# The combined projection without its normalised input, and the lower bound's factor moved to the queries

## The chip, the cores and the metric

The kernel runs on one core of a Trainium2 chip. The metric is device time in microseconds (us), the median of several runs; lower is better. Where a profile is read, it is that of a single execution. PE is the matrix engine, PEld its weight loads, DVE the vector engine, ACT the scalar engine, POOL the general engine (GpSimd), SP the engine that here only issues transfers. A letter q behind a name is that engine's queue.

## The reference

One layer of a bidirectional hybrid encoder on x (1, 512, 1024) with memory tokens (1, 256, 1024), all float32. The part that matters here is the first sub-layer:

```
h = rmsnorm(x, pre_mix_g)
aq, ak, av, hq, hf_fwd, hf_bwd, hi, hg = split_columns(h @ w_in, IN_SPLITS)
aq, ak = rmsnorm per head of 64 with q_norm_g, k_norm_g, then 2-D rotary
att = axial_gqa_attention(aq, ak, av)
# HGRN2 group, 4 heads of 128:
q = silu(hq)
f_dir = lb_dir + (1 - lb_dir) * sigmoid(zf_dir)      # forward and backward
k_dir = 1 - f_dir                                    # = (1 - lb_dir) * sigmoid(-zf_dir)
o = bidirectional_gated_scan(q, log f_fwd, log f_bwd, hi)
rec = rmsnorm(o, out_g) * silu(hg)
x = x + rmsnorm(concat(att, rec) @ w_out, post_mix_g)
```

A root-mean-square norm multiplies each row (token) of x by one number r and each column by a gain. The gain can go into the input of the projection, and r can be applied to the projection's output. Then follow a cross-attention into the memory, whose rows are normalised with mem_norm_g, and a gated MLP.

## The kernel before

Every matrix product is made of three matmuls, because both operands are held as a rounded part (hi, in code wh or hi) and a rest (lo, wl): hi by hi, hi by lo, lo by hi (`mm3`, L143 to L146). 132 units of weights of 128 x 1024 come in a fixed order, each through one raw buffer (2 of them) into wh and wl (4 buffers each). `issue` (L115) makes a unit: the plain way is a cast on ACT and a subtraction on DVE (`split`, L102); units in NEG_SCALAR (4 to 27) get a cast on ACT (L121), a negation on ACT (L123), and a second transfer of the same weights on POOL's queue that adds them to the negation (L126); units in NEG_POOL (28 to 41) are negated on POOL. `unit` (L137) hands out the next unit and issues up to AHEAD = 3 units beyond those taken; `hold` (L131) is an upper limit for that.

The instructions of each engine run in the order that a planner gave them when the kernel was built; it follows the order of the text, but an instruction that the plan sees ready earlier can be put ahead. `tc.issue_after(i)` puts instructions behind i on i's engine. `weave` (L57) mixes several streams of text by their progress.

The start, in order:

- L338 to L376: x arrives transposed in eight chunks of 128 columns, is multiplied by the gain of its columns and split into `raw_act` (the input without r), while units 0 to 3 are split; the projection of the values v (column group hi) runs on PE (L375) from `raw_act`.
- L386 to L397: ACT squares and sums the rows of x (L388), POOL makes r (`rstd_of`, L160) and multiplies the identity by it into `diag_r` (L392), PE spreads r over all partitions by multiplying with ones (L395), ACT copies that into `r_bc` (L397).
- L400: `normalize` makes the normalised input: gain and r on DVE (L402), then a split (ACT L103, DVE L104) into `hT`. It is called for chunks 0 to 7 between the matmuls of head 0 (L671 to L673).
- L439: `put_v` multiplies v's rows by r on ACT as they leave the accumulators, ahead of head 0's projections.
- `hgrn_in(h)` (L459): three projections of a head, one unit each: q (silu: L465, L466), then the gates f and the keys k of both directions (`put_f`, L468 to L476). Head 0 reads `raw_act`, and its results are multiplied by r_bc on DVE (`scaled`, L442 to L446). Heads 1 to 3 read `hT`.
- `mix_projections` (L654): `mem_norm` (L639), which loads the memory's gain and rows on POOL's queue (L157, L644), squares the rows on ACT (L197) and scales them on DVE (L179); then the projection of the output gate (`put_sg`, L449: sigmoid on ACT, the gain out_g on POOL, product on DVE), heads 1 and 2, `mem_turn`, keys and values (`put_kv`), queries (`put_qn`), head 3. With it are woven the cores 0 to 2.
- `hgrn_core(h)` (L486): the scan of a head. It begins with ksum = k_fwd + k_bwd (DVE L496) and its product with q (PE L499), and goes on in seven doubling steps, each with a copy on ACT (L506), matmuls (L509), products on DVE (L535) and a masked copy (L541), then further steps; at the end the head's output is normalised, multiplied by the gate (L559), turned and split into `mix`.

Accumulator banks go by tags of two buffers each: b (head projections), c (cores), s and o (gate, keys, queries). Sixteen large buffers of 8 KB a partition (`big`, tag big) hold activations.

Of the kernel before, what the change touches and what calls it, by code (L numbers as in the profile page):

```python
# [18 lines left out]
P = 128  # L19
# [54 lines left out]
def layer(tc, io, out):  # L74
# [30 lines left out]

    pending, last_pow = deque(), [None]
    issued, taken, last_load = [0], [0], [None]
# [35 lines left out]
    def mm3(o, a, b, start, stop):  # L143
        nc.tensor.matmul(o, a[0], b[0], start=start, stop=False)  # L144
        nc.tensor.matmul(o, a[0], b[1], start=False, stop=False)  # L145
        nc.tensor.matmul(o, a[1], b[0], start=False, stop=stop)  # L146

# [11 lines left out]

    def rstd_of(ss, n, width):  # L160
        r = small()
        nc.gpsimd.tensor_scalar(r[:, :n], ss, 1.0 / width, EPS, op0=ALU.mult, op1=ALU.add)
        last_pow[0] = nc.gpsimd.tensor_tensor(out=r[:, :n], in0=r[:, :n], in1=nhalf[:, :n], op=ALU.pow).ins
        return r
# [172 lines left out]

    raw_act = new_act()  # L338

    after = []  # L340

    def split_x(kc):
        src = xt[kc // 4][:, kc % 4, :]
        hi, lo = raw_act.get(kc, slice(0, T))
# [18 lines left out]
    for j in range(4):  # L363
        if j >= 2:
            w_raw.append(load_w())
        wh = wp.tile([P, 1024], F32R, name="wh", tag="wh")
        wl = wp.tile([P, 1024], F32R, name="wl", tag="wl")
        for k in range(2):
            in_turn(split_x, 2 * j + k)
            in_turn(split_w, wh[:, half(k)], wl[:, half(k)], w_raw[j][:, half(k)])  # L370
        for k in range(2):
            kc = 2 * j + k
            for a, w in ((0, wh), (0, wl), (1, wh)):
                for b in range(NB):
                    nc.tensor.matmul(v_ps[b], raw_act.get(kc, blk(b))[a], w[:, half(k)],  # L375
                                     start=kc == 0 and a == 0 and w is wh, stop=kc == 7 and a == 1)  # L376
# [5 lines left out]
    taken[0] = 4  # L382
    for _ in range(2):
        issue()

    rx = const.tile([P, 2 * NB], F32, name="rx")  # L386
    for b in range(NB):
        nc.scalar.activation(tmp4([P, D]), xr[b], ACT.Square, accum_out=rx[:, b:b + 1])  # L388
    r = rstd_of(rx[:, :NB], NB, D)
    diag_r = tmp2((P, NB, P), tag="th")  # L390
    for b in range(NB):
        nc.gpsimd.tensor_scalar(diag_r[:, b, :], ident, r[:, b:b + 1], None, op0=ALU.mult)  # L392
    r_ps = bank("c")
    for b in range(NB):
        nc.tensor.matmul(r_ps[:, blk(b)], ones, diag_r[:, b, :], start=True, stop=True)  # L395
    r_bc = big([P, T])
    nc.scalar.copy(r_bc, r_ps)  # L397
    hT = new_act()

    def normalize(kc):  # L400
        t = tmp2()
        nc.vector.scalar_tensor_tensor(out=t, in0=xt[kc // 4][:, kc % 4, :], scalar=gcol[:, kc:kc + 1], in1=r_bc,  # L402
                                       op0=ALU.mult, op1=ALU.mult)
# [5 lines left out]
    og = const.tile([P, P], F32, name="og")  # L409
    cw = const.tile([P, 2 * NF, 4], F32, name="cw")  # L410
    qkg = const.tile([P, 2, 64], F32, name="qkg")
    with tc.issue_after(last_load[0]):
        nc.sync.dma_start(lbt, io["hg_lb"])
        nc.sync.dma_start(og, rows_bc(io["hg_out_norm_g"], P))
# [44 lines left out]
    def hgrn_in(h, between=(), raw=False):  # L459
        qk = big([P, 2, 2, T])  # L460
# [7 lines left out]
        def put_f(d):  # L468
            def put(z):
# [3 lines left out]
                nc.scalar.activation(k, z, ACT.Sigmoid, scale=-1.0)  # L473
                nc.vector.tensor_scalar(f, f, oml[:, d, h:h + 1], lb[:, d, h:h + 1], op0=ALU.mult, op1=ALU.add)
                nc.vector.tensor_scalar(k, k, oml[:, d, h:h + 1], None, op0=ALU.mult)
# [106 lines left out]
    def norm_rope(z, nh, which, b):  # L582
        n = nh * 64
        rope = qkv["rope"]
        u = tmp2()
        nc.scalar.activation(u[:, :n], z, ACT.Square)
        ss = small()
        nc.vector.tensor_reduce(ss[:, :nh], u[:, :n].rearrange("p (h d) -> p h d", h=nh), axis=AX.X, op=ALU.add)
        r = rstd_of(ss[:, :nh], nh, 64)
        xn = tmp2()  # L590
# [7 lines left out]
        nc.vector.tensor_add(xn[:, :n], xn[:, :n], u[:, :n])  # L598
        nc.vector.tensor_tensor(out=x3, in0=x3, in1=r[:, :nh, None].to_broadcast([P, nh, 64]), op=ALU.mult)
        return x3  # L600

    def put_kv(b, z):
# [5 lines left out]
        vv = qkv["vv"]  # L608
        split(vv[:, b, :, 0, :], vv[:, b, :, 1, :], z[:, 128:256].rearrange("p (h d) -> p h d", h=2))
        kr = norm_rope(z[:, 0:128], 2, 1, b)  # L610
# [42 lines left out]

    def mix_projections():  # L654
        mem_norm()
        yield from proj_tm(hT, tm_tags, put_sg)
        yield from hgrn_in(1)
# [359 lines left out]
```

## Time and profile before

| | |
|---|---|
| median of 3 runs | 849.56 us (848.68 to 850.97) |
| the profiled execution, its own time | 848.33 us |
| its span, first to last instruction | 846.5 us |
| granted clock of PE, mean | 0.994 |
| read from memory over the span | 100.63 MB |

A row of the timeline reads: start, duration, engine, line, operation, output<-input, shapes, and in brackets the idle time before it and what ended it. A row of the groups reads: line, engine, operation, names, shapes, count, then busy time and mean nanoseconds of one, then the idle time of the engine just before and what ended most of it. A row of the waits reads: engine, tile and line that waited, what it waited for, us in total, how often, the longest. x24 is a count.

### The profile page before, as it was taken

What the parts mean: (1) busy time and instruction counts of PE and PEld (TensorE: products, weight loads), DVE (VectorE), ACT (ScalarE), POOL (GpSimd) and SP (SyncE); (2) the same over time, 40 slices, a digit from 0 to 9 for tenths busy, and PEclk for the clock granted to TensorE, in tenths of its full rate; (3) what the DMA queues carried; (4) which work ended last, traced back from release to release, by engine and by line L of the source; (5) the groups of instructions that cost most, each with busy time, mean ns of one, the idle gap of its engine ahead of it and who ended that gap; (6) DMA issues with size and microseconds to landing.
All of it is one profiled execution on the core that took longest, in us unless ns stands there. A gap on an engine that the chain in (4) does not pass through costs nothing.

```text
span 846.5 us, 11102 instructions
## 1 busy us (share of the span) xinstructions
PE 828.5 (98%) x4304; PEld 703.5 (83%) x4304; DVE 493.2 (58%) x775; ACT 424.3 (50%) x735; POOL 107.7 (13%) x166
## 2 busy tenths in 40 slices
PE   9789999999999999999999999999999999999996
PEld 7668888988999888888888998888888888888885
DVE  5277276928987675854544865555555557722224
ACT  6764555555988774645443553333333335511121
POOL 0321411225332301300001300000000000000001
PEclk9999999999999999999999999999999999999999
DMA  8985664558677633242302242222233222222212
GB/s 320 249 220 119 143 152 94 121 129 171 152 180 167 150 103 147 85 164 75 123 27 75 93 131 100 93 90 92 100 100 99 100 101 88 99 90 96 100 50 100
DMA packets 30228, 103.45 MB, mean 122 GB/s; under 512 B 3872, under 2 KB 4512, under 8 KB 30176
## 3 DMA queue, kind: packets, MB, share of 16 engines
q1 hardware_dynamic: 22752, 77.44, 27.0%
q0 software_dynamic: 6704, 24.38, 15.4%
q10 hardware_dynamic: 720, 0.92, 0.3%
q8 instruction: 34, 0.56, 0.3%
q14 instruction: 18, 0.15, 0.1%
HBM read 100.63 MB, written 2.10 MB: 121 GB/s over the span
## 4 chain that ended last, share of the span: by engine, by line
PE 91%; DMA 4%; DVE 2%; ACT 2%; POOL 1%; issue 1%; SPq 0%; POOLq 0%; DVEq 0%; ACTq 0%
PE ps_b L146 10%; PE ps_b L144 10%; PE ps_b L145 10%; PE ps_s L146 6%; PE ps_s L145 6%; PE ps_s L144 6%; PE ps_o L144 6%; PE ps_o L145 6%; PE ps_o L146 6%; PE ps_c L144 4%; PE ps_c L145 4%; PE ps_c L146 4%; PE ps_c L509 3%; PE ps_o L727 2%; PE ps_o L715 2%; PE ps_s L705 2%
## 5 line engine op out<-in xcount | busy, mean ns | idle before, releaser
L104 DVE TENSOR_TENSOR wl<-raw,wh 128x1024 fp32r<-128x1024 f32 x90 | 110.2, 1224 | 199.5 <-ACT wh L103 199.3
L103 ACT CAST wh<-raw 128x1024 fp32r<-128x1024 f32 x90 | 94.8, 1053 | 203.7 <-PE ps_o L146 71.4
L146 PE MATMUL ps_b<-big,wl 128*128 128x512 f32 (+1 forms) x320 | 117.5, 367 | 5.1 <-DMA wl<-in_w_dram 5.1
L144 PE MATMUL ps_b<-big,wh 128*128 128x512 f32 (+1 forms) x320 | 118.6, 371 | 0.0
L145 PE MATMUL ps_b<-big,wh 128*128 128x512 f32 (+1 forms) x320 | 117.1, 366 | 0.0
L146 PEld LDWEIGHTS ps_b<-big,wl 128*128 128x128 f32 x320 | 60.7, 190 | 14.8 <-DMA wl<-in_w_dram 5.5
L172 POOL TENSOR_SCALAR small<-small 128x1 f32<-128x1 f32 x40 | 14.3, 356 | 440.4 <-ACT tmp L203 421.5
L144 PEld LDWEIGHTS ps_b<-big,wh 128*128 128x128 f32 x320 | 60.8, 190 | 9.0
L145 PEld LDWEIGHTS ps_b<-big,wh 128*128 128x128 f32 x320 | 60.7, 190 | 9.1
L121 ACT CAST wh<-raw 128x1024 fp32r<-128x1024 f32 x38 | 39.9, 1051 | 32.3 <-PE ps_b L145 14.7
L144 PE MATMUL ps_s<-wh,big 128*128 128x512 f32 (+1 forms) x140 | 54.0, 386 | 0.0
L535 DVE TENSOR_TENSOR big<-big 128x512 f32<-128x512 f32 x64 | 47.0, 741 | 10.5 <-ACT tmp L506 3.7
L146 PE MATMUL ps_s<-wh,big 128*128 128x512 f32 (+1 forms) x140 | 53.1, 379 | 0.0
L145 PE MATMUL ps_s<-wl,big 128*128 128x512 f32 (+1 forms) x140 | 53.0, 379 | 0.0
L144 PE MATMUL ps_o<-wh,big 128*128 128x512 f32 (+1 forms) x124 | 48.1, 388 | 0.0
L126 POOL DMA_DIRECT2D wl<-in_w_dram x38 | 34.2, 901 | 109.0 <-ACT wl L123 99.0
L146 PE MATMUL ps_o<-wh,big 128*128 128x512 f32 (+1 forms) x124 | 47.5, 383 | 0.0
L145 PE MATMUL ps_o<-wl,big 128*128 128x512 f32 (+1 forms) x124 | 47.3, 381 | 0.0
L104 DVE TENSOR_TENSOR big<-ps_o,big 128x512 fp32r<-128x512 f32 x52 | 35.8, 689 | 15.4 <-ACT big L103 15.1
L103 ACT CAST big<-ps_o 128x512 fp32r<-128x512 f32 x52 | 30.4, 585 | 21.3 <-PE ps_o L715 7.9
L509 PE MATMUL ps_c<-big,tmp 128*128 128x128 f32 x224 | 32.8, 289 | 4.4 <-ACT tmp L506 4.0
L144 PE MATMUL ps_b<-wh,big 128*128 128x512 f32 x92 | 36.6, 398 | 0.0
(250 smaller groups left out, 1964.2 us busy)
## 6 DMA issues: line engine op xcount, KB each, us to landing
raw<-in_w_dram SPq DMA_DIRECT2D x131, 512.0 KB, 3.3
wl<-in_w_dram POOLq DMA_DIRECT2D x38, 512.0 KB, 5.5
big<-in_x_dram SPq DMA_DIRECT2D x8, 512.0 KB, 8.0
big<-in_xt_dram SPq DMA_DIRECT2D x3, 512.0 KB, 7.6
big<-in_mem_dram POOLq DMA_DIRECT2D x2, 512.0 KB, 10.9
out_dram<-big SPq DMA_DIRECT2D x4, 256.0 KB, 2.1
out_dram<-big ACTq DMA_DIRECT2D x3, 256.0 KB, 2.1
big<-in_xt_dram SPq DMA_DIRECT2D x2, 256.0 KB, 4.0
```

Of the source, the lines that this page charges most:

```text
L103: nc.scalar.copy(hi, src)
L104: (eng or nc.vector).tensor_sub(lo, src, hi.bitcast(F32))
L121: nc.scalar.copy(wh, raw)
L126: nc.gpsimd.dma_start(wl, io["w"][i], accum_op=ALU.add)
L144: nc.tensor.matmul(o, a[0], b[0], start=start, stop=False)
L145: nc.tensor.matmul(o, a[0], b[1], start=False, stop=False)
L146: nc.tensor.matmul(o, a[1], b[0], start=False, stop=stop)
L509: nc.tensor.matmul(o[:, b, :], kc[:, blk(b)], pat(qk, b * P, [[2 * m, P // (2 * m)], [T + m, 2], [1, m]]), start=True, stop=True)
L535: nc.vector.tensor_tensor(out=c, in0=c, in1=pat(tt, toff + off, [[2, npair], [gap, 2], [0, m]]), op=ALU.mult)
L705: nc.tensor.matmul(s, qT[h // 4][:, h % 4, blk(qb)], kT[:, 2 * (h // 4) + c, :], start=c == 0, stop=c == 1)
L715: nc.tensor.transpose(o[:, c, :], e[:, 0, blk(c)], ident)
L727: nc.tensor.matmul(o, vv[:, c, h // 4].rearrange("p a d -> p (a d)"), pt[:, j, c, :], start=c + j == 0, stop=c == 3 and j == 1)
```

## The change

- `raw_act` is now called `hT` and is the only input of the combined projection; `normalize` and the second, normalised activation are gone. Everything that reads the projection applies r itself: v, the gate (scale of the sigmoid, and a factor of the product), values (`split_scaled`), the rotary norm (r goes into the square's scale and into the norm's factor, one more POOL operation), and all four heads through `scaled`, not head 0 alone.
- diag_r is multiplied on DVE, not on POOL. The spreading of r is put behind the 18th matmul of head 0's first projection (SPREAD_STEP = 2). `put_v` comes after it.
- Units 4, 5 and 6 are split by ACT and DVE; NEG_SCALAR begins at 7. Units 6 and 7 are issued behind the copy of r_bc.
- The keys k keep no factor 1 - lb. That factor (`oml`) goes to q times f, and into ksum. The gate f = lb + oml * sigmoid is formed on ACT. Half of ksum is a multiplication on ACT.
- The gain out_g leaves the gate; it is applied per partition when the head's output is split into `mix`.
- `mem_norm` comes after the gate's projection.

```diff
-NEG_SCALAR = frozenset(range(4, 28))
+NEG_SCALAR = frozenset(range(7, 28))
...
-WARM = 4
+WARM, SPREAD_STEP = 4, 2
...
+    def split_scaled(hi, lo, src, factor):
+        nc.scalar.mul(hi, src, factor)
+        nc.vector.scalar_tensor_tensor(out=lo, in0=src, scalar=factor, in1=hi.bitcast(F32), op0=ALU.mult,
+                                       op1=ALU.subtract)
...
-    raw_act = new_act()
+    hT = new_act()
...
     taken[0] = 4
-    for _ in range(2):
-        issue()
+    hold[0] = 6
+    issue_ahead()
...
-    r = rstd_of(rx[:, :NB], NB, D)
+    r = rstd_of(rx[:, :NB], NB, D, rx[:, NB:])
     diag_r = tmp2((P, NB, P), tag="th")
     for b in range(NB):
-        nc.gpsimd.tensor_scalar(diag_r[:, b, :], ident, r[:, b:b + 1], None, op0=ALU.mult)
-    r_ps = bank("c")
-    for b in range(NB):
-        nc.tensor.matmul(r_ps[:, blk(b)], ones, diag_r[:, b, :], start=True, stop=True)
+        nc.vector.tensor_scalar(diag_r[:, b, :], ident, r[:, b:b + 1], None, op0=ALU.mult)
     r_bc = big([P, T])
-    nc.scalar.copy(r_bc, r_ps)
-    hT = new_act()
-
-    def normalize(kc):
-        t = tmp2()
-        nc.vector.scalar_tensor_tensor(out=t, in0=xt[kc // 4][:, kc % 4, :], scalar=gcol[:, kc:kc + 1], in1=r_bc,
-                                       op0=ALU.mult, op1=ALU.mult)
-        split(*hT.get(kc, slice(0, T)), t)
+
+    def spread_r():
+        r_ps = bank("c")
+        with tc.issue_after(last_mm[0]):
+            for b in range(NB):
+                nc.tensor.matmul(r_ps[:, blk(b)], ones, diag_r[:, b, :], start=True, stop=True)
+        copied = nc.scalar.copy(r_bc, r_ps).ins
+        hold[0] = N_UNITS
+        with tc.issue_after(copied):
+            issue_ahead()
+        for b in range(NB):
+            put_v(b, v_ps[b])
...
-        nc.scalar.activation(s, o, ACT.Sigmoid)
-        s4 = s.rearrange("p (h n) -> p h n", h=4)
-        nc.gpsimd.tensor_tensor(out=s4, in0=s4, in1=og[:, None, :].to_broadcast([P, 4, P]), op=ALU.mult)
-        nc.vector.tensor_mul(sg_box[0][:, b, :], o, s)
+        nc.scalar.activation(s, o, ACT.Sigmoid, scale=r[:, b:b + 1])
+        nc.vector.scalar_tensor_tensor(out=sg_box[0][:, b, :], in0=o, scalar=r[:, b:b + 1], in1=s,
+                                       op0=ALU.mult, op1=ALU.mult)
...
-                nc.vector.tensor_scalar(f, f, oml[:, d, h:h + 1], lb[:, d, h:h + 1], op0=ALU.mult, op1=ALU.add)
-                nc.vector.tensor_scalar(k, k, oml[:, d, h:h + 1], None, op0=ALU.mult)
-                nc.vector.tensor_mul(qk[:, 0, 1 - d, :], q, f)
+                nc.scalar.activation(f, f, ACT.Identity, scale=oml[:, d, h:h + 1], bias=lb[:, d, h:h + 1])
+                nc.vector.scalar_tensor_tensor(out=qk[:, 0, 1 - d, :], in0=f, scalar=oml[:, d, h:h + 1], in1=q,
+                                               op0=ALU.mult, op1=ALU.mult)
...
-            yield from proj_fm(raw_act if raw else hT, T, "b", scaled(put) if raw else put)
+            yield from proj_fm(hT, T, "b", scaled(put))
...
-        nc.vector.tensor_add(ksum, qk[:, 1, 0, :], qk[:, 1, 1, :])
+        nc.scalar.mul(ksum, qk[:, 1, 0, :], oml[:, 0, h:h + 1])
+        nc.vector.scalar_tensor_tensor(out=ksum, in0=qk[:, 1, 1, :], scalar=oml[:, 1, h:h + 1], in1=ksum,
+                                       op0=ALU.mult, op1=ALU.add)
...
-        split(*mix.get(4 + h, slice(0, T)), o.rearrange("p b n -> p (b n)"))
+        split_scaled(*mix.get(4 + h, slice(0, T)), o.rearrange("p b n -> p (b n)"), og[:, 0:1])
...
-        nc.scalar.activation(u[:, :n], z, ACT.Square)
+        nc.scalar.activation(u[:, :n], z, ACT.Square, scale=r[:, b:b + 1])
...
-        r = rstd_of(ss[:, :nh], nh, 64)
+        rz = rstd_of(ss[:, :nh], nh, 64)
+        nc.gpsimd.tensor_scalar(rz[:, :nh], rz[:, :nh], r[:, b:b + 1], 0.0, op0=ALU.mult, op1=ALU.add)
...
     def mix_projections():
-        mem_norm()
         yield from proj_tm(hT, tm_tags, put_sg)
+        mem_norm()
         yield from hgrn_in(1)
...
-    for b in range(NB):
-        put_v(b, v_ps[b])
-    for i, _ in enumerate(hgrn_in(0, raw=True)):
-        if i < KC:
-            normalize(i)
+    for i, _ in enumerate(hgrn_in(0)):
+        if i == SPREAD_STEP:
+            spread_r()
```

More of the change, by code (lines that the diff above doesn't have):

```diff
@@ L104, in split @@
         (eng or nc.vector).tensor_sub(lo, src, hi.bitcast(F32))
-    pending, last_pow = deque(), [None]
+    def split_scaled(hi, lo, src, factor):
+        nc.scalar.mul(hi, src, factor)
+        nc.vector.scalar_tensor_tensor(out=lo, in0=src, scalar=factor, in1=hi.bitcast(F32), op0=ALU.mult,
+                                       op1=ALU.subtract)
+    pending, last_pow, last_mm = deque(), [None], [None]
     issued, taken, last_load = [0], [0], [None]
@@ L145, in mm3 @@
         nc.tensor.matmul(o, a[0], b[1], start=False, stop=False)
-        nc.tensor.matmul(o, a[1], b[0], start=False, stop=stop)
+        last_mm[0] = nc.tensor.matmul(o, a[1], b[0], start=False, stop=stop).ins
     def blk(b):
@@ L158, in gains, with rstd_of @@
         return [g[:, i, :] for i in range(len(names))]
-    def rstd_of(ss, n, width):
-        r = small()
+    def rstd_of(ss, n, width, r=None):
+        r = small() if r is None else r
         nc.gpsimd.tensor_scalar(r[:, :n], ss, 1.0 / width, EPS, op0=ALU.mult, op1=ALU.add)
@@ L343, in split_x @@
         src = xt[kc // 4][:, kc % 4, :]
-        hi, lo = raw_act.get(kc, slice(0, T))
+        hi, lo = hT.get(kc, slice(0, T))
         cast = nc.scalar.mul(hi, src, gcol[:, kc:kc + 1]).ins
@@ L374, in layer @@
                 for b in range(NB):
-                    nc.tensor.matmul(v_ps[b], raw_act.get(kc, blk(b))[a], w[:, half(k)],
+                    nc.tensor.matmul(v_ps[b], hT.get(kc, blk(b))[a], w[:, half(k)],
                                      start=kc == 0 and a == 0 and w is wh, stop=kc == 7 and a == 1)
@@ L408, in layer @@
     lbt = const.tile([P, 2, 2, 4], F32, name="lbt")
-    og = const.tile([P, P], F32, name="og")
+    og = const.tile([P, 1], F32, name="og")
     cw = const.tile([P, 2 * NF, 4], F32, name="cw")
@@ L413, in layer @@
         nc.sync.dma_start(lbt, io["hg_lb"])
-        nc.sync.dma_start(og, rows_bc(io["hg_out_norm_g"], P))
+        nc.sync.dma_start(og, io["hg_out_norm_g"][:, None])
         nc.sync.dma_start(masks_f, io["masks"])
@@ L452, in put_sg, with hgrn_in @@
         s = tmp2()
-        nc.scalar.activation(s, o, ACT.Sigmoid)
-        s4 = s.rearrange("p (h n) -> p h n", h=4)
-        nc.gpsimd.tensor_tensor(out=s4, in0=s4, in1=og[:, None, :].to_broadcast([P, 4, P]), op=ALU.mult)
-        nc.vector.tensor_mul(sg_box[0][:, b, :], o, s)
+        nc.scalar.activation(s, o, ACT.Sigmoid, scale=r[:, b:b + 1])
+        nc.vector.scalar_tensor_tensor(out=sg_box[0][:, b, :], in0=o, scalar=r[:, b:b + 1], in1=s,
+                                       op0=ALU.mult, op1=ALU.mult)
         sg_box.append(b)
-    def hgrn_in(h, between=(), raw=False):
+    def hgrn_in(h, between=()):
         qk = big([P, 2, 2, T])
@@ L598, in norm_rope @@
         nc.vector.tensor_add(xn[:, :n], xn[:, :n], u[:, :n])
-        nc.vector.tensor_tensor(out=x3, in0=x3, in1=r[:, :nh, None].to_broadcast([P, nh, 64]), op=ALU.mult)
+        nc.vector.tensor_tensor(out=x3, in0=x3, in1=rz[:, :nh, None].to_broadcast([P, nh, 64]), op=ALU.mult)
         return x3
@@ L608, in put_kv @@
         vv = qkv["vv"]
-        split(vv[:, b, :, 0, :], vv[:, b, :, 1, :], z[:, 128:256].rearrange("p (h d) -> p h d", h=2))
+        split_scaled(vv[:, b, :, 0, :], vv[:, b, :, 1, :], z[:, 128:256].rearrange("p (h d) -> p h d", h=2), r[:, b:b + 1])
         kr = norm_rope(z[:, 0:128], 2, 1, b)
@@ L654, in mix_projections @@
     def mix_projections():
+        yield from proj_tm(hT, tm_tags, put_sg)
         mem_norm()
-        yield from proj_tm(hT, tm_tags, put_sg)
         yield from hgrn_in(1)
```

## The prediction

> **What bounds the kernel now.** I read the page's first part, then PE's waits, then busy time by stage (in that view each row has the stretch and its length, then the busy time of PE, PE's weight loads, DVE, ACT and POOL, the granted clock, the share of the transfer engines and GB/s).
>
> ```profile
> span 846.5 us, 11102 instructions
> PE 828.5 (98%) x4304; PEld 703.5 (83%) x4304; DVE 493.2 (58%) x775; ACT 424.3 (50%) x735; POOL 107.7 (13%) x166
> ...
> PE ps_b L146 <- DMA wl<-in_w_dram: 5.1, 1, 5.1
> PE ps_c L509 <- ACT tmp L506: 4.0, 2, 3.6
> ```
> ```profile
> 0.00:20.00 20.00, 18.52 (x70) 14.70 (x70) 10.27 (x17) 12.33 (x21) 0.44 (x6) 1.00 0.88 320
> ...
> 20.00:300.00 280.00, 270.18 (x1651) 236.47 (x1650) 191.90 (x383) 188.64 (x345) 79.22 (x95) 0.99 0.67 156
> 300.00:800.00 500.00, 500.00 (x2414) 419.90 (x2413) 274.84 (x356) 213.62 (x351) 24.06 (x53) 1.00 0.29 100
> 800.00:846.00 46.00, 39.80 (x175) 32.38 (x173) 16.22 (x21) 9.73 (x20) 4.01 (x12) 0.97 0.22 78
> ```
> PE is busy 98% of the span, and from 300 to 800 us without a gap at full clock. The change leaves the number and the size of the matmuls as they are, so time can be won only where PE stands still or runs at a low clock. The stage from 20 to 300 us has 9.8 us of idle PE (280.00 - 270.18), and two waits make nearly all of it: 5.1 us for a transferred wl, and 3.6 us for a copy on ACT. The 6.2 us after 800 us are the output, which the change does not touch. So less work on DVE, ACT or POOL is worth nothing by itself: the question is what becomes of the two waits. PE's timeline around them:
>
> ```profile
> 27.93 1.05 PE L395 MATMUL ps_c<-tmp,ones 128*128 128x128 f32 x8
> 28.74 0.48 PE L144 MATMUL ps_b<-big,wh 128*128 128x512 f32 x1
> ...
> 34.51 0.80 PE L146 MATMUL ps_b<-big,wl 128*128 128x512 f32 x1 [5.06 <-DMA wl<-in_w_dram]
> ...
> 37.67 0.39 PE L144 MATMUL ps_b<-big,wh 128*128 128x512 f32 x1
> ...
> 51.76 0.39 PE L146 MATMUL ps_b<-big,wl 128*128 128x512 f32 x1
> 51.99 0.39 PE L144 MATMUL ps_s<-wh,big 128*128 128x512 f32 x1
> ...
> 55.85 1.16 PE L499 MATMUL ps_c<-tmp,tmp 128*128 128x128 f32 x8
> 60.61 1.73 PE L509 MATMUL ps_c<-big,tmp 128*128 128x128 f32 x8 [3.60 <-ACT tmp L506]
> 62.00 0.77 PE L146 MATMUL ps_o<-wh,big 128*128 128x512 f32 x1
> ...
> 65.06 0.40 PE L144 MATMUL ps_s<-wh,big 128*128 128x512 f32 x1
> ...
> 69.58 1.13 PE L509 MATMUL ps_c<-big,tmp 128*128 128x128 f32 x8 [0.41 <-ACT tmp L506]
> ```
> At full clock a 512-column matmul starts 0.227 us after the one before it (51.76 to 51.99, and so for dozens of rows). **Wait 1.** Head 0's three projections have 3 x 24 = 72 matmuls, 16.3 us at that pace; they take 51.99 - 28.74 = 23.25 us. So wait 1 costs 6.9 us: 5.06 us of standing, about 1.6 us for seven matmuls at a slow clock (34.51 to 37.67 is 3.16 us, where 7 x 0.227 = 1.59), and a remainder. **Wait 2.** It costs 3.60 us, plus 0.6 us (1.73 against the 1.13 us that the same eight passes take at 69.58), plus 62.00 to 65.06 for seven matmuls, 3.06 - 1.59 = 1.47: 5.7 us. Together 12.6 us. The short wait at 69.58 (0.41 us) is followed by the normal pace: only the long ones cost the clock too.
>
> Now what makes them, on ACT and POOL:
>
> ```profile
> 23.34 0.20 POOL L162 TENSOR_SCALAR small<-rx 128x4 f32<-128x4 f32 x1 [22.37 <-ACT tmp L388]
> 23.63 1.03 POOL L163 TENSOR_TENSOR small<-small,nhalf 128x4 f32<-128x4 f32 x1
> ...
> 27.08 1.03 POOL L126 DMA_DIRECT2D wl<-in_w_dram  x1
> ...
> 47.25 0.85 POOL L126 DMA_DIRECT2D wl<-in_w_dram  x1 [8.50 <-ACT wl L123]
> ...
> 48.36 0.85 POOL L644 DMA_DIRECT2D big<-in_mem_dram x1
> ```
> ```profile
> 23.51 1.05 ACT L121 CAST wh<-raw 128x1024 fp32r<-128x1024 f32 x1 [0.26 <-DMA raw<-in_w_dram]
> 24.59 1.06 ACT L123 ACTIVATE wl<-wh 128x1024 fp32r<-128x1024 f32 x1
> 26.30 1.05 ACT L121 CAST wh<-raw 128x1024 fp32r<-128x1024 f32 x1 [0.66 <-DMA raw<-in_w_dram]
> ...
> 58.68 1.06 ACT L197 ACTIVATE tmp<-big 128x1024 f32<-128x1024 f32 x1 [3.66 <-DMA big<-in_mem_dram]
> 59.64 0.19 ACT L197 ACTIVATION_READ_ACCUMULATOR tmp<-big 128x1 f32 x1
> 59.74 0.82 ACT L506 COPY tmp<-big 128x512 f32<-128x512 f32 x1
> ```
> Wait 1: unit 4 makes its wl by a negation on ACT (L123) and a second, adding transfer on POOL's queue (L126); that starts at 27.08, after the POOL multiplications of diag_r, and lands at 34.5. Wait 2: ACT works in order; the square of the memory rows (L197) stands ahead of core 0's first copy (L506) and waits for rows that were asked for at 48.36.
>
> **The change, part by part.** Transfers and durations that I use:
>
> ```profile
> DMA to landing us min/median/max: 7.4/8.5/9.2
> ```
> ```profile
> DMA to landing us min/median/max: 5.3/5.7/10.4
> ```
> ```profile
> raw<-in_w_dram SPq DMA_DIRECT2D x17, 512.0 KB, 5.3
> ```
> ```profile
> L104 DVE TENSOR_TENSOR wl<-raw,wh 128x1024 fp32r<-128x1024 f32 x90 | 110.2, 1224 | 199.5 <-ACT wh L103 199.3
> ```
> ```profile
> L402 DVE SCALAR_TENSOR_TENSOR tmp<-big,gcol 128x512 f32<-128x512 f32 x8 | 5.7, 749 | 3.5 <-ACT big L397 3.5
> L474 DVE TENSOR_SCALAR big<-big,oml,lb 128x512 f32<-128x512 f32 x8 | 5.1, 635 | 10.0 <-ACT big L472 10.0
> L475 DVE TENSOR_SCALAR big<-big,oml 128x512 f32<-128x512 f32 x8 | 3.8, 481 | 0.0
> L445 DVE TENSOR_TENSOR tmp<-ps_b,big 128x512 f32<-128x512 f32 x3 | 2.1, 690 | 3.9 <-PE ps_b L146 3.9
> ```
> ```profile
> L440 ACT ACTIVATE big<-ps_o,small 128x512 f32<-128x512 f32 x2 | 1.4, 696 | 0.0
> ```
> The first two rows are the landing times of wl's adding transfers: the three asked for from 20 to 34 us, and all thirteen up to 110 us.
>
> *Units 4 to 6 leave the adding transfer.* Unit 4's wh is ready at 23.51 + 1.05 = 24.6, its wl after DVE's subtraction (1.22) at 25.8, before the v projection ends at 27.9. Unit 5: 26.30 + 1.05 + 1.22 = 28.6. Wait 1 goes: -6.9. What hides the 3 x 1.22 us on DVE is idle time there: 3.5 us of it stand in the row of L402, whose first instruction waits for L397. What is late next? PE runs unit 4 from 27.9, with the spreading of r (0.8 us, 28.74 - 27.93, as before) behind its 18th matmul at 32.0. That needs diag_r: r at 23.63 + 1.03 = 24.7, four DVE multiplications of at most 0.64 each (L474 is four times as wide): 27.2, no wait. Unit 5 begins at 34.2, unit 6 at 39.6, unit 7 at 45.1. Units 6 and 7 are now cast behind r_bc's copy on ACT (queued behind that copy: both casts, then put_v), which ends at about 33.5. Unit 6: cast to 34.5, subtraction to 35.8, in good time. Unit 7 keeps the adding transfer: its raw buffer is free when unit 5's subtraction ends (28.6), the load takes 5.3 (33.9), cast and negation end at 36.7, and it lands 5.7 later at 42.4, or at 45.9 by the 9.2 of the crowded rows: between 2.7 us early and 0.8 late. Unit 8: buffer free at 35.8, loaded 41.1, negated 43.2, landed 48.9 to 52.4, wanted at 45.1 + 5.45 = 50.6: 1.7 early to 1.8 late. I take 0.5 for both and keep 0 to 2.6. I lean to the lower end because the three crowding transfers of 27 to 35 us are gone; a stall of this length would not cost the clock (69.58).
> The Trainium skill ("DMA: Bandwidth & Descriptors", Anatomy of one DMA — SWDGE (gpsimd) path) gives such a transfer about 2.0 us plus its bytes over 436 GB/s, an estimate of 3.2 us for 512 KB, and by it this term would be 0. The trace does not bear that out: the shortest of the thirteen took 5.3.
>
> *No second, normalised activation.* Eight multiplications (0.75), eight casts and eight subtractions go from 33 to 52 us, some 11 us of DVE and 5 of ACT. None was on the path of PE: worth 0 by itself, but head 0's chain from its last matmul to ksum no longer queues behind them. Four big buffers fall away; r_bc is kept until head 3.
>
> *Heads 1 to 3 are scaled on DVE.* Three more multiplications each (0.69), against two L474 and two L475 less (2 x 0.64 + 2 x 0.48 = 2.2): DVE even. ACT gets two affine gates and half of ksum per head, 3 x 0.70 by the row of L440 (0.6 to 0.8): 8.4 us over four heads, beside PE's 24 matmuls a unit. The chain to L499 gains a DVE step and loses two. PE reads ahead two banks of ps_b, which DVE now frees. I take 0.3 for small waits (0 to 1.5). Queued behind a late gate on ACT are L506's copies, for which PE would wait as in wait 2.
>
> *Output gate, gains, rotary.* put_sg's product on POOL goes, one small POOL operation per norm_rope comes (below 0.5 us, eight times, in a chain beside PE): 0. og loads one column: 0.
>
> *mem_norm behind the gate projection.* Its three loads (1.5 MB) and two squares leave the start of core 0. Wait 2 goes: -5.7. What is late then is only the chain from unit 6's last matmul to ksum: scaling 0.69, two sigmoids and a sum, about 2.7 us, with the gate projection's matmuls on PE meanwhile. But the loads and squares come at least 22 us later (four units of 5.45), with core 0 near its end, whose copies then stand behind a square on ACT. Bounds: 0, if the rows have landed, and 5.7, if it repeats. The gate's evacuations no longer need POOL, and ps_b no longer waits for ACT, so fewer of PE's next matmuls hang on ACT than at wait 2. I take 1.0.
>
> Sum: 848.3 (the profiled execution: span 846.5 and 1.8 around it) - 6.9 - 5.7 + 0.5 + 0.3 + 1.0 = 837.5. It stands 1.2 below the median of 849.56, so for the median: **838.7**.
>
> **The rivals.**
> *The memory wait comes back later.* For it: ACT stays in order, and the rows shown landed late:
>
> ```profile
> DMA to landing us min/median/max: 10.3/10.9/11.4
> ```
> Against it: that was at a time of full transfer engines, and PE has the next head's 72 matmuls queued. Then 5.7 instead of 1.0: about 843.4. Chance 0.2.
>
> *Units 7 and 8 late for long*: put_v and the sigmoid of head 0 slip before unit 7's cast on ACT (4 x 0.70 + 0.6), so 3.4 us on top of the 0.8 late: a stall above 3 us with a slow clock, 5.7 as in wait 2: 844. Chance 0.08.
>
> *The memory loads go first: slower.* In the kernel before, all 16 big buffers belong to tiles opened before mem_norm; POOL stood idle for 22.37 us ahead of L162 and did not load them. In the changed kernel only 14 are opened ahead of them, so nothing in the data holds their loads back, and their squares on ACT with them. At 320 GB/s (0 to 20 us) they put 4.9 us before the first weights, and ACT, in order, would wait 10.9 + 2.1: up to 17.9, more than the 12.6 won, so slower: 855. It decides if ACT is held at the start for more than 12.6 us in all. Against it: the schedule before issued nothing of it even in POOL's 8.50 us of idle time ahead of 47.25, after x's row buffers were free. Chance 0.08.
>
> *It does not do what it says*: the two waits stay because another transfer or buffer ends last in the same places, 848 to 851. Chance 0.05.
>
> **How the numbers follow.** The forecast, give-back of 0 to 4.1 us, has 0.59: 836.9 to 841.0. The range takes in the memory rival and, below, the 1.2 us of idle PE that are left in that stage (9.8 - 5.06 - 3.60): 835.5 to 844.5, with about 0.85 of the cases. A measurement of this kernel tells 0.3%, 2.5 us, from no change. Faster: 0.87; within: 0.05; slower: 0.08.
>
> **What would show it.** PE's wait for wl at L146 and for L506 gone from the first 65 us; sg's first matmul near 45 instead of 51.99; granted clock 1.00 from 30 to 65 us; idle PE from 20 to 300 us below 4 us; the rest of the kernel shifted and of equal length. I am wrong if ACT's wait for in_mem_dram returns with PE behind it, if the first matmul of the v projection starts later than now, or if units 7 or 8 show PE waits above 2 us.

## The result, and where the time went

The changed kernel takes 845.06 us (median; 844.64 to 846.16) against 848.68 us (847.95 to 850.97) of the kernel before on the same chip: ratio 0.9962, interval 0.9949 to 0.9975. It is faster by 3.6 us, where 838.7 was forecast, and it lies 0.6 us above the stated range of 835.5 to 844.5. The profiled execution took 846.16 us, its span 844.3.

The early part came as forecast. Page and PE timeline of the changed kernel (its lines are shifted: projections L149 to L151, scaling L451, first copy of a core L513 with matmuls L516, split L103/L104 and L126 to L131 as L121 to L126 before):

```profile
span 844.3 us, 11078 instructions
PE 828.5 (98%) x4304; PEld 703.4 (83%) x4304; DVE 488.2 (58%) x759; ACT 427.7 (51%) x736; POOL 102.4 (12%) x163
```
```profile
27.86 0.39 PE L380 MATMUL ps_o<-wh,big 128*128 128x512 f32 x1
28.08 0.39 PE L149 MATMUL ps_b<-big,wh 128*128 128x512 f32 x1
...
45.33 0.39 PE L149 MATMUL ps_s<-wh,big 128*128 128x512 f32 x1
...
55.75 0.51 PE L516 MATMUL ps_c<-big,tmp 128*128 128x128 f32 x2 [0.49 <-ACT tmp L513]
...
181.99 0.39 PE L149 MATMUL ps_b<-big,wh 128*128 128x512 f32 x1
```

Busy PE is the same 828.5 us; the 2.2 us that the span lost are idle time. Unit 4 starts with no wait at 28.08; the gate's first matmul comes at 45.33 instead of 51.99; what is left of wait 2 is 0.49 us. Head 3's first matmul is at 181.99, where the kernel before has

```profile
191.43 0.39 PE L144 MATMUL ps_b<-big,wh 128*128 128x512 f32 x1
```

So the change is 9.4 us ahead there, and 2.2 us ahead at the end: 7.2 us were given back in between, nearly all of it by the output of core 3 (its first matmul is at 271.65, before at 273.83). Ahead of head 3 some 2.1 us had gone already: at head 1's first matmul the lead is 11.6 us (81.14 against 92.72), and then PE waits 0.19 us at 105.52, 0.83 at 130.73 and 1.03 at 147.66. Two windows of each kernel (columns as in the prediction's rows by stage), and the changed kernel's PE timeline with its waits, show where the 7.2 us went:

```profile
180.00:200.00 20.00, 20.00 (x106) 16.84 (x105) 12.65 (x23) 11.73 (x23) 9.72 (x11) 1.00 0.74 173
200.00:220.00 20.00, 19.67 (x123) 17.07 (x123) 17.07 (x30) 13.93 (x24) 7.69 (x8) 1.00 0.69 145
```
```profile
180.00:200.00 20.00, 19.44 (x91) 16.02 (x89) 11.41 (x18) 10.38 (x13) 10.11 (x12) 1.00 0.74 162
200.00:220.00 20.00, 15.97 (x114) 15.16 (x114) 18.21 (x30) 15.36 (x27) 7.31 (x9) 0.91 0.60 129
```
```profile
205.50 0.54 PE L637 MATMUL ps_s<-ident_r,tmp 128*128 128x128 f32 x4 [1.89 <-DVE tmp L104]
205.88 0.50 PE L637 MATMUL ps_o<-ident_r,tmp 128*128 128x128 f32 x4
208.50 0.38 PE L149 MATMUL ps_b<-big,wh 128*128 128x256 f32 x1 [2.12 <-DVE tmp L451]
...
210.60 0.41 PE L150 MATMUL ps_b<-big,wh 128*128 128x256 f32 x1
210.81 0.41 PE L151 MATMUL ps_b<-big,wl 128*128 128x256 f32 x1
```

The first two rows are the kernel before, the next two the changed one: from 200 to 220 us PE is idle 4.0 us instead of 0.3, and the clock falls to 0.91. PE waits to turn the normalised queries (L637, for their split on DVE) and for the scaled projection of head 3 (L451), and then starts its 256-column matmuls 0.21 us apart (210.60 to 210.81) instead of 0.12 (201.42 to 201.54). What made both late is seen at the first norm of the queries. In the changed kernel these are the last matmul of the first block of queries, the first scaling of head 3 and the first square of a norm; in the kernel before, the same matmul and the square:

```profile
177.19 0.39 PE L151 MATMUL ps_s<-wh,big 128*128 128x512 f32 x1
```
```profile
187.63 0.69 DVE L451 TENSOR_TENSOR tmp<-ps_b,big 128x512 f32<-128x512 f32 x1 [7.87 <-PE ps_b L151]
```
```profile
188.36 0.68 ACT L593 ACTIVATE tmp<-ps_s,rx 128x512 f32<-128x512 f32 x1
```
```profile
186.64 0.39 PE L146 MATMUL ps_s<-wh,big 128*128 128x512 f32 x1
```
```profile
188.22 1.28 ACT L586 ACTIVATE tmp<-ps_s 128x512 f32<-128x512 f32 x2
```

The first square of the q norms (`put_qn`, L593) comes at 188.36, as late as before, though PE is 9.4 us earlier: block 0 of the queries had its last matmul at 177.19, and DVE stood idle for 7.87 us. In the kernel before the square followed its matmul (186.64) in 1.6 us. In the text, the four norms are called *behind* head 3's projections, two behind the first and two behind the second, and their temporaries are of tag ta, which has four buffers. The change opens one more of that tag ahead of them: z of head 3, which is written only when its projection is done.

### The profile page after: what moved, and what is told of

Its sections match the earlier page's. It is cut to its first block, busy times and chain, and to the rows that moved or that the text cites. A ratio compares the mean times of both kernels' runs of the same rounds, so it can differ in the third digit from the quotient of the medians.

```text
span 844.3 us, 11078 instructions
## 1 busy us (share of the span) xinstructions
PE 828.5 (98%) x4304; PEld 703.4 (83%) x4304; DVE 488.2 (58%) x759; ACT 427.7 (51%) x736; POOL 102.4 (12%) x163
## 4 chain that ended last, share of the span: by engine, by line
PE 91%; DVE 3%; ACT 2%; DMA 2%; POOL 1%; issue 1%; POOLq 0%; DVEq 0%; ACTq 0%
PE ps_b L149 9%; PE ps_b L150 9%; PE ps_b L151 9%; PE ps_s L151 6%; PE ps_s L149 6%; PE ps_s L150 6%; PE ps_o L149 6%; PE ps_o L151 6%; PE ps_o L150 6%; PE ps_c L149 4%; PE ps_c L150 4%; PE ps_c L151 4%; PE ps_c L516 3%; PE ps_o L733 2%; PE ps_s L711 2%; PE ps_o L721 2%
## 5 line engine op out<-in xcount | busy, mean ns | idle before, releaser
L104 DVE TENSOR_TENSOR wl<-raw,wh 128x1024 fp32r<-128x1024 f32 x93 | 113.8, 1224 | 199.9 <-ACT wh L103 199.8
L103 ACT CAST wh<-raw 128x1024 fp32r<-128x1024 f32 x93 | 97.9, 1053 | 206.2 <-PE ps_o L151 71.4
L149 PE MATMUL ps_b<-big,wh 128*128 128x512 f32 (+1 forms) x320 | 118.6, 371 | 2.1 <-DVE tmp L451 2.1
L151 PE MATMUL ps_b<-big,wl 128*128 128x512 f32 (+1 forms) x320 | 117.3, 367 | 0.0
L149 PEld LDWEIGHTS ps_b<-big,wh 128*128 128x128 f32 x320 | 61.0, 191 | 11.3 <-DVE tmp L451 2.3
L151 PEld LDWEIGHTS ps_b<-big,wl 128*128 128x128 f32 x320 | 60.9, 190 | 9.3
L149 PE MATMUL ps_s<-wh,big 128*128 128x512 f32 (+1 forms) x140 | 54.1, 387 | 0.0
L151 PE MATMUL ps_s<-wh,big 128*128 128x512 f32 (+1 forms) x140 | 53.3, 381 | 0.0
L126 ACT CAST wh<-raw 128x1024 fp32r<-128x1024 f32 x35 | 36.7, 1048 | 30.3 <-PE ps_o L151 16.1
L149 PE MATMUL ps_o<-wh,big 128*128 128x512 f32 (+1 forms) x124 | 47.9, 386 | 0.0
L151 PE MATMUL ps_o<-wh,big 128*128 128x512 f32 (+1 forms) x124 | 46.7, 377 | 0.0
L131 POOL DMA_DIRECT2D wl<-in_w_dram x35 | 31.2, 892 | 112.9 <-ACT wl L128 103.3
L104 DVE TENSOR_TENSOR big<-ps_o,big 128x512 fp32r<-128x512 f32 x52 | 35.7, 688 | 15.1 <-ACT big L103 14.9
L103 ACT CAST big<-ps_o 128x512 fp32r<-128x512 f32 x52 | 30.3, 586 | 19.6 <-PE ps_o L830 7.5
L149 PE MATMUL ps_b<-wh,big 128*128 128x512 f32 x92 | 36.7, 399 | 0.0
L150 PE MATMUL ps_b<-wl,big 128*128 128x512 f32 x92 | 36.2, 393 | 0.0
```

Of the source, the lines that this page charges most:

```text
L103: nc.scalar.copy(hi, src)
L104: (eng or nc.vector).tensor_sub(lo, src, hi.bitcast(F32))
L126: nc.scalar.copy(wh, raw)
L131: nc.gpsimd.dma_start(wl, io["w"][i], accum_op=ALU.add)
L151: last_mm[0] = nc.tensor.matmul(o, a[1], b[0], start=False, stop=stop).ins
```

## The experiments

T1: the buffers of a tag are given out in the order in which the text opens them, and that holds the norms back behind z. T2: large buffers are short, because r_bc keeps one until head 3. T3: the added work itself is too much for the stretch.

| kernel | us, median | ratio to the kernel before, interval |
|---|---|---|
| changed | 845.06 | 0.9962 (0.9949 to 0.9975) |
| x1: changed, z of head 3 in tag th | 838.14 | 0.9874 (0.9859 to 0.9889) |
| x2: changed, r_bc beside the rope tables | 845.85 | 0.9966 (0.9954 to 0.9978) |
| x3: changed, head 3 unscaled | 838.66 | 0.9878 (0.9861 to 0.9895) |
| x4: before, both early moves | 839.24 | 0.9889 (0.9875 to 0.9903) |
| x5: before, units 4 to 6 split | 848.47 | 0.9996 (0.9987 to 1.0004) |
| x6: before, mem_norm later | 844.22 | 0.9947 (0.9934 to 0.9959) |
| x7: x1, gates on DVE | 835.99 | 0.9851 (0.9836 to 0.9866) |
| x8: changed, norms ahead of z in the text | 838.68 | 0.9883 (0.9868 to 0.9897) |
| x9: changed, gates on DVE | 848.34 | 0.9990 (0.9980 to 1.0000) |
| x10: x4, with z of head 3 | 851.09 | 1.0025 (1.0017 to 1.0034) |
| x11: x7, memory turned in banks s and o | 836.12 | 0.9849 (0.9835 to 0.9864) |
| x12: x1, only f on DVE | 837.63 | 0.9866 (0.9853 to 0.9879) |

**x1, z of head 3 in another tag.**

```diff
-    def scaled(put):
+    def scaled(put, tag):
         def use(o):
-            z = tmp2()
+            z = tmp2(tag=tag)
...
-            yield from proj_fm(hT, T, "b", scaled(put))
+            yield from proj_fm(hT, T, "b", scaled(put, "th" if h == 3 else "ta"))
```


> The changed kernel, with the scaled projection z of head 3 taken from the temporaries of tag th (idle at that time) instead of those of tag ta, which the four q norms use as well. Nothing is left out. Theory T1 (the q norms, opened in the text behind z of head 3, wait for that z although their own projection is done 10 us earlier): the first square of a q norm comes near 178 us instead of 188.36, the two waits of 1.89 and 2.12 us on DVE at 205 to 208 us go, so do the cold matmuels behind them (16 of 256 columns at 0.213 instead of 0.119 us, 1.5 us), and the time falls by 4.5 to 7 us from the changed kernel's 845.1, to 838 to 840.5. Theory T2 (a large buffer is short because r_bc keeps one of 16 until head 3): no change, 845 within 0.8. Theory T3 (the added scaling work on DVE and the added step on GpSimd are too much for the stretch, whenever it starts): no change or at most 1.5 us less, 843.5 to 845.5.

838.14 us. The squares come 10.7 us earlier, at 177.62, the waits at 205 to 208 us are gone, and the clock is 1.00 from 20 to 300 us:

```profile
177.62 1.26 ACT L593 ACTIVATE tmp<-ps_s,rx 128x512 f32<-128x512 f32 x2
```
```profile
200.00:220.00 20.00, 19.16 (x145) 18.10 (x145) 18.30 (x37) 18.35 (x35) 6.44 (x6) 1.00 0.62 145
```

All the scaling and the added GpSimd steps are still there, so T3 falls; 6.9 us hung on the tag's name. Not all of them lie behind the late norms: x1 starts head 3 at 180.74 instead of 181.99, mostly because it lacks the wait of 1.03 us at 147.66. x2 below lacks that wait too, with z in tag ta, so it is not shown that the tag makes it.

**x2, r_bc without a large buffer of its own.**

```diff
-    r_bc = big([P, T])
+    rope_box = big([P, 2048])
+    r_bc = rope_box[:, 1536:2048]
...
-        both = big([P, 6, NB, 64])
+        both = rope_box[:, 0:1536].rearrange("p (i b n) -> p i b n", i=6, b=NB)
```


> The changed kernel, with r_bc placed in the unused quarter of the large buffer of the rope tables, so that it takes no large buffer of its own (16 at most instead of 17 wanted). Nothing is left out. T2 (large buffers short): the waits at 205 and 208 us go, 838 to 840.5. T1 (z of head 3 holds the q norms back) and T3 (added work): the waits at 205.5 and 208.5 us stay, 845 within 0.8.

845.85 us, the same waits of 1.9 and 2.1 us: T2 falls.

**x3, head 3 without its z.**

```diff
-            yield from proj_fm(hT, T, "b", scaled(put))
+            yield from proj_fm(hT, T, "b", scaled(put) if h < 3 else put)
```


> The changed kernel, but head 3 reads its three projections from the PSUM banks without multiplying by r_bc, as the kernel before reads all of heads 1 to 3. This leaves the normalising factor out of head 3 (part of the computation). It takes away the three multiplications of 0.68 us and the temporaries z. T1: the same gain as with z in its own tag, 838 to 840.5, within 1 us of that run. T3: this gains (3 x 0.68 us of DVE work less in the stretch, 2 us or more), while z in its own tag does not. T2: no change, 845 within 0.8.

838.66 us, 0.5 from x1, within the spread of the two. Taking the three multiplications away brings nothing that moving the tile does not.

**x8, the same tag in another order of the text.**

```diff
-    def scaled(put):
+    def scaled(put, jobs):
         def use(o):
+            for job in jobs:
+                job()
             z = tmp2()
...
-            yield from proj_fm(hT, T, "b", scaled(put))
-            for job in between[:2]:
-                job()
+            yield from proj_fm(hT, T, "b", scaled(put, between[:2]))
             between = between[2:]
```


> The changed kernel with everything still in tag ta, but the text calls two q norms ahead of opening each z of head 3 instead of behind it. Nothing is left out. T1 (the order in which the tag is opened is the order in which it is given): the q norms start near 178 us, and now the z of head 3 stand behind them: z of the first gate waits for the norms of blocks 2 and 3. That costs less than the 10 us of late norms, 838.5 to 842. If only the waits of z itself (2.12 us, last gate) mattered and not the start of the norms: no gain, 844 to 846.

838.68 us, and the norms start 10.3 us earlier than in the change:

```profile
178.05 1.26 ACT L593 ACTIVATE tmp<-ps_s,rx 128x512 f32<-128x512 f32 x2
```

Nothing but the order in the text differs from the change, and the tag has the same four buffers, so it is the order, and not the number of buffers, that held the norms back. By which step it does so the traces do not tell: in the changed kernel the first square also stands right behind a weight cast on ACT that had itself waited 3.07 us for PE (187.40), so it may have waited for its buffer or have been put late in ACT's planned order.

**x10, the cause put into the other kernel.** Beside this edit it has both early moves, shown below for x4.

```diff
+    def copied(put):
+        def use(o):
+            z = tmp2()
+            nc.vector.tensor_copy(z, o)
+            put(z)
+        return use
...
-            yield from proj_fm(raw_act if raw else hT, T, "b", scaled(put) if raw else put)
+            yield from proj_fm(raw_act if raw else hT, T, "b", scaled(put) if raw else copied(put) if h == 3 else put)
```


> The kernel before with the two early moves (839.2 us), and with the suspected cause put into it: the three projections of head 3 are copied on VectorE to a temporary of tag ta before their use, where the kernel before reads the bank. Nothing is left out. T1 (z in the tag of the q norms holds these back): the first square of a q norm goes from near 178 to near 188 us, and the time rises by 4 to 7 us to 843 to 846. T3 (work of the projections' scaling): three copies of under 0.7 us are hidden as in the run with z in tag th, 839 to 840.

851.09 us, 11.9 more than x4; the direction is T1's, the size nearly twice what I expected. The signature is that of the change, an idle DVE ahead of z and the first square right behind it (in x4 it comes at 178.82):

```profile
189.18 0.69 DVE L452 COPY tmp<-ps_b 128x512 f32<-128x512 f32 x1 [8.03 <-PE ps_b L146]
```
```profile
189.91 0.59 ACT L593 ACTIVATE tmp<-ps_s 128x512 f32<-128x512 f32 x1
```

Three copies of 0.69 us are 2.1 us of work, and work of that size was hidden in x1. The size goes with the place of the gates: they are on DVE here, and x9 against x7 (below), which also differ only in z's tag and have the gates on DVE, is 12.4 us, where the change against x1, with gates on ACT, is 6.9.

**x4, x5, x6: the two early moves without the new projection.** x5 is the first edit alone, x6 the second, x4 both, on the kernel before.

```diff
-NEG_SCALAR = frozenset(range(4, 28))
+NEG_SCALAR = frozenset(range(7, 28))
...
-        mem_norm()
         yield from proj_tm(hT, tm_tags, put_sg)
+        mem_norm()
```


> The kernel before with only the two moves that take the two early waits away: NEG_SCALAR from unit 7, and mem_norm behind the gate projection. No part of the unnormalised projection. Nothing is left out. If the two early waits are worth what the prediction gave them (6.9 and 5.7 us) and the rest of the change brings nothing, 836 to 838; T1 and T3 both expect no waits near 205 to 208 us here, since heads 1 to 3 have no z. Against it: head 0 of the kernel before normalises eight tiles on DVE and ScalarE while units 4 to 6 would now be split there too, so those may come late; then 840 to 846.

> The kernel before with NEG_SCALAR from unit 7 and nothing else: weight units 4 to 6 are split on ScalarE and VectorE instead of having their low part added by DMA. Nothing is left out. The prediction's price for this wait was 5.06 us plus the cold clock behind it, 6.9 in all; run alone it should bring 842 to 843.5. Rival: head 0's projection of the kernel before also waits for nothing else, but its eight tiles are normalised on VectorE at the same time, so three more splits there delay something else and only 2 to 5 us remain, 844 to 847.

> The kernel before with mem_norm behind the gate projection in the text and nothing else. Nothing is left out. The prediction's price for the second wait was 3.60 us plus the cold clock behind it, 5.7 in all: 843 to 844.5. Rival: the sum of the keys of head 0 is late on VectorE anyway (in the run with both moves it still kept TensorE waiting 2.56 us), so that this move alone brings no more than 1 to 4 us: 845 to 848.

x4 839.24, x5 848.47, x6 844.22 us. Only x6 lies where the price had put it; x5 is above both its ranges and x4 between them. The values do not add: 0.3 us alone, not told from nothing, and 4.6 alone make 9.8 together, each against the kernel before as timed beside it. x5 shows why, in PE's timeline and on ACT:

```profile
53.29 1.71 PE L499 MATMUL ps_c<-tmp,tmp 128*128 128x128 f32 x8 [2.54 <-DVE tmp L496]
...
66.50 2.05 PE L509 MATMUL ps_c<-big,tmp 128*128 128x128 f32 x8 [6.54 <-DVE big L535]
```
```profile
59.96 1.06 ACT L197 ACTIVATE tmp<-big 128x1024 f32<-128x1024 f32 x1 [7.05 <-DMA big<-in_mem_dram]
```

With wait 1 gone PE reaches core 0 earlier, but the memory rows land no earlier (their first square starts at 59.96, before at 58.68), and ACT now stands 7.05 us for them instead of 3.66. The 5.06 us of wait 1 come back as 2.54 for the keys' sum and 6.54 instead of 3.60 for wait 2; here a product on DVE (L535) ends that wait, which stood behind the scaling of the same rows (L179). The first of these stays when mem_norm has moved (x4):

```profile
52.61 1.16 PE L499 MATMUL ps_c<-tmp,tmp 128*128 128x128 f32 x8 [2.56 <-DVE tmp L496]
```

There DVE still normalises eight chunks. Its busy time from 28 to 65 us is the third figure behind the length, x4 first, then x1, which has no second activation:

```profile
28.00:65.00 37.00, 34.05 (x172) 28.26 (x171) 29.22 (x49) 26.63 (x38) 5.62 (x6) 1.00 0.73 183
```
```profile
28.00:65.00 37.00, 36.02 (x183) 30.05 (x182) 18.90 (x35) 25.17 (x34) 4.81 (x6) 1.00 0.69 178
```

29.22 against 18.90 us, and the wait is 0.58 us in x1. x7 below, whose gates are formed on DVE as in x4, starts the same sum at 48.40 us instead of 51.87. So dropping that activation seems to earn something, but only once the other waits are out of its way; no run dropped it alone.

**x7, x9, x12: the gates.** x7 and x9 undo the gate part of the change, x7 in x1, x9 in the change itself; x12 undoes only its first line, in x1.

```diff
-                nc.scalar.activation(f, f, ACT.Identity, scale=oml[:, d, h:h + 1], bias=lb[:, d, h:h + 1])
-                nc.vector.scalar_tensor_tensor(out=qk[:, 0, 1 - d, :], in0=f, scalar=oml[:, d, h:h + 1], in1=q,
-                                               op0=ALU.mult, op1=ALU.mult)
+                nc.vector.tensor_scalar(f, f, oml[:, d, h:h + 1], lb[:, d, h:h + 1], op0=ALU.mult, op1=ALU.add)
+                nc.vector.tensor_scalar(k, k, oml[:, d, h:h + 1], None, op0=ALU.mult)
+                nc.vector.tensor_mul(qk[:, 0, 1 - d, :], q, f)
...
-        nc.scalar.mul(ksum, qk[:, 1, 0, :], oml[:, 0, h:h + 1])
-        nc.vector.scalar_tensor_tensor(out=ksum, in0=qk[:, 1, 1, :], scalar=oml[:, 1, h:h + 1], in1=ksum,
-                                       op0=ALU.mult, op1=ALU.add)
+        nc.vector.tensor_add(ksum, qk[:, 1, 0, :], qk[:, 1, 1, :])
```


> The changed kernel with z of head 3 in tag th, and with the gates as in the kernel before: f and the factor 1 - lower bound on the keys formed on VectorE, the sum of the keys in one VectorE addition. Nothing is left out. VectorE gets two instructions of 0.90 and two of 0.47 us more per head and ScalarE three of 0.72 to 0.81 less. If moving the gates to ScalarE is worth nothing in itself: 838 within 0.8. If VectorE is what keeps TensorE waiting in head 0 and head 3: the wait for the sum of the keys near 52 us grows from 0.58 to 1.5 to 3, and 839 to 841.

> The changed kernel with only its gate part undone (f, the factor on the keys and the sum of the keys on VectorE as in the kernel before), z of head 3 in tag ta as in the change. Nothing is left out. If the cost of the gate part (2.15 us, found beside the early norms) and that of z's tag (6.9 us) are separate: 842.3 to 843.5, and the q norms still start near 186 to 188. If with late norms the added VectorE work of 1 us per head stands in the same queue and takes the gain back: 844.5 to 846.

> The changed kernel with z of head 3 in tag th, and only the gate's multiply and add (f) back on VectorE; the factor stays on the query side and ScalarE still forms half of the keys' sum. Nothing is left out. VectorE gets two instructions of about 0.55 us per head, ScalarE two of 0.80 less. If the length of ScalarE's queue ahead of f is what costs: most of the 2.15 us comes back, 836 to 837. If it is the half of the keys' sum (0.72 us, queued behind the weights of 1.05 us): 837.5 to 838.5.

x7 835.99, x9 848.34, x12 837.63 us. x7 and x9 came as neither theory had it. With the norms in time, the gates on DVE are 2.15 us *better*, where I had asked whether they are equal or worse. Head 0's sum of the keys in x1 (ACT, then DVE) and in x7 (DVE) shows one part of it:

```profile
49.68 1.05 ACT L128 ACTIVATE wl<-wh 128x1024 fp32r<-128x1024 f32 x1
50.63 0.71 ACT L501 ACTIVATE tmp<-big,oml 128x512 f32<-128x512 f32 x1
```
```profile
51.55 0.74 DVE L502 SCALAR_TENSOR_TENSOR tmp<-big,oml,tmp 128x512 f32<-128x512 f32 x1
```
```profile
48.40 0.69 DVE L501 TENSOR_TENSOR tmp<-big 128x512 f32<-128x512 f32 x1
```

The half on ACT queues behind a weight of 1.05 us and the sum is done 3.2 us later (52.29 against 49.09), with the wait of 0.58 us on PE. At 213.83 x1 also has a wait of 0.77 us for the softmax that x7 lacks. x12 keeps half of the sum on ACT and gets 0.5 us of the 2.15, within the spread of x1. That is what was expected if the sum is what costs; but x12 loses the waits at 52 and 213 us and gains one of 1.81 at 139.96, so it does not tell the two halves apart.

With the norms late it is the other way round: x9 is 3.3 us *worse* than the change, though it is 2.0 us ahead when z of head 3 is scaled (185.67 against 187.63). The two waits for the late norms are still there (2.08 and 2.24 us), and three more come behind them:

```profile
216.98 1.40 PE L709 MATMUL ps_s<-big 128*128 128x512 f32 x4 [0.87 <-ACT tmp L690]
219.38 1.32 PE L719 MATMUL ps_o<-ident,tmp 128*128 128x128 f32 x8 [0.99 <-ACT tmp L695]
220.98 0.50 PE L709 MATMUL ps_s<-big 128*128 128x512 f32 x1 [0.28 <-ACT tmp L690]
```

As I read it, PE has by then used up the filler between the scores: it ran 23 of the 256-column matmuls at the low clock before 212 us, the changed kernel 16. (The low clock lasted 6.8 us in x9, twice as long as in the change; but it did so in x2 too, which is only 0.8 us slower than the change.) x10 has the same two first waits (0.87 and 0.99 us), and it has the gates on DVE too. So the gates on ACT take 3.3 us off a stall of which z's tag is the cause, and cost 2.15 us where there is no stall. Why the plan left no filler there in the one and left some in the other was not tried.

**x11, one more wait.**

```diff
-            turn_in(kv["rows"][:, b, :], kv["m"], b, "bb")
+            turn_in(kv["rows"][:, b, :], kv["m"], b, "so")
```


> The kernel with z of head 3 in tag th and the gates on VectorE (836.0 us), with the turned memory rows in the banks s and o, which are idle there, instead of bank b, which still holds the last projection of head 2. Nothing is left out. The wait of 1.09 us at 129.5 us goes: 834.6 to 835.4. If the k and v projection behind it then waits for the same banks: 836 or more.

836.12 us: nothing. The wait of 1.09 us went, and two of 0.47 and 0.27 us came in its place at 129.5 and 130.3 us; x7 remains the best, 12.8 us below the kernel before.

## Why the prediction was wrong, step by step

- **Wait 1, -6.9: came.** The gate's first matmul is 6.66 us earlier. But the price was that of a wait with nothing behind it: alone the edit brings 0.3 us (x5). It counted because wait 2 was removed with it.
- **Wait 2, -5.7: came**, as far as 0.49 us. Alone it brings 4.6 (x6). Together, on the kernel before, 9.8 of the 12.6 (x4), with 2.56 left as a wait for the keys' sum.
- **Units 7 and 8, +0.5: 0.** No PE wait for a wl is in the changed trace, though the five adding transfers asked for from 37 to 55 us took 5.5 to 8.7 us to land.
- **The memory rows, +1.0: 0.** Their squares run at 82.56 and 83.85 us with no wait for a transfer; that rival, at 0.2, did not happen.
- **"No second, normalised activation … worth 0 by itself": nearly.** By the DVE times above it keeps the keys' sum from being 2.56 us late once both waits are gone. x1 against x4 is 1.1 us, x7 against x4, with the same gates, 3.25; both differences hold the rest of the change too.
- **"Heads 1 to 3 are scaled on DVE … DVE even … I take 0.3 for small waits (0 to 1.5)": this is the step that failed.** I counted instructions of 0.69 us and engine time, and that sum was right: with z in another tag the work is hidden (x1 and x3 agree within 0.5 us). I did not count the temporary that each multiplication opens, nor ask who opens the same tag after it in the text. It cost up to 6.9 us: 4.0 us of PE standing between 203.6 and 208.5 us, about 1.5 us for 16 matmuls at the slow pace behind them, and smaller waits, of which the 1.03 us at 147.66 may have another cause. The small waits that this term was meant for came to some 2.1 us before head 3, above its bound of 1.5, too.
- **ACT's gates** stood in the same 0.3. Their ACT time (9.3 us by the rows of the changed kernel, eight of 0.806 and four of 0.718, where I took 8.4) is beside PE, as I said, but the chain through ACT is worth 2.15 us in x1 against x7, and the sign turns with the norms (x9).

The forecast for a kernel without the tag's effect would have been near: x1, which has every other part of the change, takes 838.14 us against 838.7. That is partly luck. The sum took 12.6 us for the two waits and gave back 1.8; in the runs the two moves bring 9.8, and the rest of the change, with z out of the way, adds 1.1, as the difference of some 3.25 won and 2.15 lost. Nearly the same total comes from other terms. Of the list of what would show it, the waits (but for the 0.49 us), the gate's first matmul and the clock from 30 to 65 us came as written. Idle PE from 20 to 300 us is about 7.6 us, not below 4, and the rest is not just shifted: the stretch from head 3's first matmul to its core's output is 7.3 us longer.

## What to carry to other kernels

A new temporary can cost more than the instruction that fills it: find its tag, and list who opens a buffer of that tag behind it in the text and runs beside it in time, since those wait for it however early their data are ready. Two waits in a row on one engine are not two prices; ask of each what it would be worth alone, and what the next one is tied to (here a transfer that lands no earlier when PE is earlier). When a saving shows up in the first half of a trace and not at the end, compare the lead at one instruction after another, and look for an engine that stands idle just ahead of the place where it shrinks.

## What the runs showed of the hardware

The clock did not go by the longest wait. In the changed kernel waits of 1.89 and 2.12 us with 0.88 us of work between 204 and 208 us brought it to 0.60 from 208 to 212; a single wait of 2.56 us in x4 left it at 1.00, and so did 1.81 us in x12:

```profile
204.00:208.00 4.00, 0.88 (x8) 0.74 (x8) 4.00 (x8) 1.84 (x3) 3.59 (x4) 1.00 0.96 157
208.00:212.00 4.00, 3.50 (x17) 3.51 (x18) 3.38 (x6) 3.12 (x5) 0.28 (x1) 0.60 0.94 222
```

The granted clock was at 0.50 for 3.4 us, from 208.76 to 212.18; in x2, with the same two waits (1.88 and 2.12 us), for 6.8 us, from 207.27 to 214.10. The Trainium skill ("TensorE: Matmul & The Clock Gate", Part 1: The HAM clock gate) says that a free-running window of about 3.4 us is watched and that the clock halves after an idle one. The halved clock and the lengths of one and two windows agree, and nearly so the pace (0.21 against 0.12 us). A window that is mostly idle was enough: the longest unbroken idle time was 2.12 us.

The multiply and add of a gate, 128 x 512 from and to the same on-chip buffer, took 0.806 us on ACT (L479 of the changed kernel) and 0.543 on DVE (L479 of x7), so moving it to ACT frees DVE and makes this step of the chain 0.26 us longer.
